# The start of the normed activations: from a multiple of 256 bytes to 192 bytes behind one

## Chip, cores and metric

The kernel runs on one core of one Trainium2 chip. The metric is the device time of one execution in microseconds; lower is better. A profile is taken in an execution of its own.

## What is computed

The reference is a decoder trunk of two layers on 256 tokens of width 1024, in float32. Each layer adds four blocks to x, each behind an RMS norm and with a second RMS norm on its output: a SwiGLU FFN (inner width 2816), a mixer, a cross-attention to 256 memory rows, and a second FFN. Layer 0 mixes with RWKV-7 (8 heads of 64) and retention (4 heads of 128) side by side, layer 1 with top-k sparse latent attention and a short convolution.

```python
for l in range(2):
    h = swiglu(rms_norm(x, ng[0]), w_gate[l, 0], w_up[l, 0], w_down[l, 0])
    x = x + 0.5 * rms_norm(h, ng[1])
    h = mixer(rms_norm(x, ng[2]))            # l = 0: rwkv7 | retention, l = 1: dsa | short conv
    x = x + rms_norm(h, ng[3])
    h = memory_xattn(rms_norm(x, ng[4]), rms_norm(mem, mem_norm_g), wq[l], wk[l], wv[l], wo[l])
    x = x + rms_norm(h, ng[5])
    h = swiglu(rms_norm(x, ng[6]), w_gate[l, 1], w_up[l, 1], w_down[l, 1])
    x = x + 0.5 * rms_norm(h, ng[7])
```

## The kernel before

Weights come from HBM in pieces of 512 KB (128 partitions x 1024 float32) into tiles wst. Each piece is split into two float32r tiles: whi, a copy by ScalarE (lines 196 and 239), and wlo, the rest wst - whi by VectorE (lines 197 and 245). Activations are split in the same way (split, lines 248 to 250). A product of two such pairs is three matmuls, hi x hi, hi x lo and lo x hi, into one PSUM bank (mm3, lines 254 to 256; project, lines 427 and 432, writes the same three in another order). Every matmul has a stationary operand of 128 columns, which a weight load brings in, and a moving operand of up to 512 columns.

The normed activations are called h here, and are the pair hhi, hlo, each 128 partitions x 8 k-tiles x 256 tokens of float32r. new_h (line 118) makes them. The class rms (line 313) fills them: it squares, scales, transposes in blocks of 128 x 128 (trh, line 351) and splits the result into hhi and hlo. There is one h for each norm ahead of a block, in the pools keep, memp, norm and hm. new_h is also called for o, the output of the cross-attention's values, and for y, the mixers' output; these take the place of an h in the pool keep.

h is read in two ways. group_t and proj_t hold the weights: whi or wlo, 128 of 256 columns, is stationary and a k-tile of h, 256 tokens, is moving. This is so for the FFNs' gate and up (pg, pu) in nine groups of 256 columns for each FFN, for the even mixer's input (pin), the memory keys (pk) and the convolution's inputs (pch, pcc, pcb). project, proj_nat and nat_both hold the activations: 128 tokens of a k-tile of h are stationary and 512 columns of weights (456 for pdi) are moving. This is so for the first 512 columns of each FFN's gate and up, for pq, pdi, prq, prv, prg and pvm. The FFN's down products (pd) and the output products (po) hold the act tiles, y or o and move 512 columns of weights.

In a group of an FFN (ffn, line 474) PE does 96 matmuls for gate and up and then 24 pd of the group before, while ScalarE and VectorE split the six weight pieces of the next ones. The weight loads are issued by SyncE as the staging tiles become free. Outside the stretches written under in_order, the tile framework orders each engine's instructions.

In the program's allocation all tiles of h, of the weights and of act start at a multiple of 256 bytes within the partition; below, such a multiple is called a line. A k-tile of h is 1024 bytes and a weight slice of 128 columns 512 bytes, so every operand of the matmuls above starts on a line. The one exception is pdi: its weight pieces have rows of 456 columns, so that the second k-tile of a piece starts 1824 bytes in, 32 bytes behind a line.

In the RWKV part front(c) handles one of four chunks of 64 tokens. It writes kr (line 948), which is squared on ScalarE and read for kn (line 963); later it writes bt (line 973) from kn, which BK reads (line 977). kr and bt have one buffer each, used by all four chunks in turn.

Of the kernel before, what the change touches and what calls it, by code (L numbers as in the profile page):

```python
# [10 lines left out]
F32 = mybir.dt.float32  # L11
F32R = mybir.dt.float32r
# [5 lines left out]
P = 128  # L18
S = 256
D = 1024  # L20
DT = D // P
# [73 lines left out]
def tile_hybrid_trunk(ctx: ExitStack, tc: tile.TileContext, a: dict, out: bass.AP, stop=None):  # L95
# [4 lines left out]
    keep = pool("keep")  # L100
# [8 lines left out]
    def bank(tag, name):  # L109
        return psum.tile([P, 512], F32, name=name, tag=tag)  # L110
# [4 lines left out]
    hneg = keep.tile([P, 4], F32, name="hneg")  # L115
    ones = keep.tile([P, 32], F32, name="ones")[:, 0:1]

    def new_h(p):
        return p.tile([P, DT, S], F32R, name="hhi", bufs=1), p.tile([P, DT, S], F32R, name="hlo", bufs=1)


    dram = pool("dram", space=bass.MemoryType.DRAM)
# [125 lines left out]
    def split(src, hi, lo):  # L248
        nc.scalar.activation(hi, src, AF.Copy)  # L249
        nc.vector.tensor_sub(lo, src, f32(hi))  # L250
# [50 lines left out]
    def power(dst, src, n):  # L301
        nc.gpsimd.tensor_tensor(dst, src, hneg[:, :n], op=ALU.pow)
# [294 lines left out]
    def cross(l, sp, y, w_unit, w_out, kts):  # L597

        wq, wo = a["xa_wq"][l], a["xa_wo"][l]
        wg, wu = a["ffn_w_gate"][l, 1], a["ffn_w_up"][l, 1]  # L600
        sc = 128.0 ** -0.5
        h, h2 = new_h(sp), new_h(sp)
        cx = ExitStack()
        xp = cx.enter_context(tc.tile_pool(reuse_waits="tile", name=f"xa{l}", bufs=1))
# [30 lines left out]
        with behind(env["loaded"]):  # L635
            nc.sync.dma_start(kT.rearrange("p a b -> p (a b)"), kd[l])
            nc.sync.dma_start(vM.rearrange("p a b -> p (a b)"), vd[l])
        gp2 = ng(l, 5)
        o = new_h(keep)
        pq, qn, qT, pr, mx, sm, pT, sps, nb = [{} for _ in range(9)]  # L640

        def query(t):
# [202 lines left out]
    def even_mixer(l, h, mh, mem_scope):  # L845
        i2 = l // 2
        w_in, w_out = a["ev_w_in"][i2], a["ev_w_out"][i2]
        with ExitStack() as cx:
            mp = cx.enter_context(tc.tile_pool(reuse_waits="tile", name="mix", bufs=1))
# [80 lines left out]
            t4 = lambda name, bufs=1: mp.tile([P, 4, 64], F32, name=name, bufs=bufs)  # L930
# [5 lines left out]
            def front(c):  # L936
                cs = slice(c * 64, (c + 1) * 64)
                inc = t4("inc")
                nc.vector.tensor_tensor_scan(fl(inc), fl(scan), fl(sig[:, c]), 0.0, op0=ALU.mult, op1=ALU.add)
                exc = mp.tile([P, 4, 64], F32, name="exc", tag="exc")  # L940
                nc.vector.tensor_sub(fl(exc), fl(inc), fl(sig[:, c]))
                e1, e2, e3 = t4("e1", 4), t4("e2"), t4("e3")
                nc.scalar.activation(e1, inc, AF.Exp, scale=-DECAY)
                nc.scalar.activation(e2, exc, AF.Exp, scale=-DECAY)
                nc.scalar.activation(e3, inc, AF.Exp, scale=DECAY)

                kr = t4("kr")
                nc.vector.tensor_mul(kr, kk[:, :, cs], pv[:, pvo["k_k"]:pvo["k_k"] + 4, None].to_broadcast([P, 4, 64]))
                sq = t4("sqk")
                nc.scalar.activation(sq, kr, AF.Square)  # L950
                ps = bank("fr", "prb")
                for f in range(4):
                    for hp, r in halves:
                        nc.tensor.matmul(ps[r, 256 + f:257 + f], sq[r, f, :], ones[r, :], start=True, stop=True)
                ssk = small.tile([P, 4], F32, name="ssk")
                nc.vector.tensor_scalar(ssk, ps[:, 256:260], 1e-24, None, op0=ALU.max)
                rin = small.tile([P, 4], F32, name="rin")
                power(rin, ssk, 4)
                dg = mp.tile([P, 4, 64], F32, name="dg", tag="sqk")
                nc.vector.tensor_mul(dg, idb, rin[:, :, None].to_broadcast([P, 4, 64]))  # L960
                nc.tensor.matmul(ps[:, 0:256], bones, fl(dg), start=True, stop=True)
                kn = t4("kn")
                nc.vector.tensor_mul(fl(kn), ps[:, 0:256], fl(kr))
                k2 = t4("k2")
                for f in range(4):
                    nc.scalar.activation(k2[:, f, :], av[:, c, f, :], AF.Identity, bias=omka[:, f:f + 1],
                                         scale=col("k_a", f))
                nc.vector.tensor_mul(k2, k2, kk[:, :, cs])
                KR = mp.tile([P, 4, 2, 64], F32, name="KR", bufs=4)
                nc.vector.tensor_mul(KR[:, :, 0, :], kn, e2)  # L970
                nc.vector.tensor_mul(KR[:, :, 1, :], rT[:, :, cs], e1)
                bt = t4("bt")
                nc.vector.scalar_tensor_tensor(fl(bt), fl(kn), -1.0, fl(e3), op0=ALU.mult, op1=ALU.mult)
                BK = mp.tile([P, 4, 2, 64], F32, name="BK")
                for hp, r in halves:
                    nc.vector.tensor_mul(BK[r, :, hp, :], k2[r], e3[r])
                    nc.vector.tensor_mul(BK[r, :, 1 - hp, :], bt[r], av[r, c])

                rk = mp.tile([P, 4, 64], F32, name="rk", tag="exc")
                nc.vector.tensor_mul(rk, rT[:, :, cs], k2)  # L980

                Q = mp.tile([P, 2, 4, 2, 64], F32, name="Q", bufs=4)
                for hp, r in halves:
                    ps = bank("fr", "pQ")
                    for f in range(4):
                        nc.tensor.matmul(ps[:, f * P:(f + 1) * P], fl(BK[r, f]), fl(KR[r, f]), start=True, stop=True)
                    nc.vector.tensor_mul(Q[:, hp].rearrange("p a k b -> p a (k b)"),
                                         ps.rearrange("p (a n) -> p a n", a=4),
                                         fl(cm)[:, None, :].to_broadcast([P, 4, P]))

                BKn = mp.tile([P, 4, P], F32, name="BKn", bufs=4)
                ps = bank("fr", "pBK")
                for f in range(4):
                    nc.tensor.transpose(ps[:, f * P:(f + 1) * P], fl(BK[:, f]), ident)
                nc.scalar.activation(fl(BKn), ps, AF.Copy)
                bn = small.tile([P, 4], F32, name="bn", bufs=4)
                ps = bank("fr", "pbn")
                for f in range(4):
                    for hp, r in halves:
                        nc.tensor.matmul(ps[r, f:f + 1], rk[r, f, :], col("r_k", f)[r, :], start=True, stop=True)  # L1000
                nc.vector.tensor_copy(bn, ps[:, 0:4])
                return e1, KR, Q, BKn, bn
# [144 lines left out]

            Sst = None
            fr = [front(i) for i in range(2)]
            U = [inverse(0, [z[2] for z in fr])]  # L1150
            for grp in (4, 5):
                shifted(grp)
            VV = [values(i) for i in range(4)]
            fr += [front(i) for i in range(2, 4)]
            U.append(inverse(1, [z[2] for z in fr[2:]]))
            for c in range(4):
# [8 lines left out]
            if mem_scope is not None:  # L1165
                mem_scope.close()
            y = retention(l, h, ya, cx)
        def w_unit(kt):
            if kt >= 4:
# [7 lines left out]
    def retention(l, h, ya, cx):  # L1177
# [54 lines left out]
        for t in range(2):  # L1232
            gates.append(r2("sgr"))
            nc.scalar.activation(fl(gates[t]), pss[t], AF.Silu)
        y = new_h(keep)
        split(ya, y[0][:, 0:4, :], y[1][:, 0:4, :])
        kv0 = r2("kv0")
        ps = bank("iv", "pkv")
        for i in range(4):
            o = slice(i * P, (i + 1) * P)  # L1240
# [3 lines left out]
        for t in range(2):  # L1244
            ps = bank("iv", "por")
            for i in range(4):
                o = slice(i * P, (i + 1) * P)
# [20 lines left out]
        for t in range(2):  # L1268
# [5 lines left out]
            o = (slice(None), slice(4, 8), slice(t * P, (t + 1) * P))  # L1274
# [4 lines left out]
    def odd_mixer(l, h, pss):  # L1279
        i2 = l // 2  # L1280
        w_in, w_out = a["od_w_in"][i2], a["od_w_out"][i2]
        with ExitStack() as cx:
# [60 lines left out]
            for t in range(2):  # L1343
                ts = slice(t * P, (t + 1) * P)
                n = (t + 1) * P
# [3 lines left out]
                for hh in range(0, 8, nb):  # L1349
# [7 lines left out]
                    for i in range(nb):  # L1357
                        k = order[hh + i]
# [18 lines left out]
                nc.vector.tensor_add(am[:, t * P:n], am[:, t * P:n], ntri)  # L1377
                amask.append(am)

            y = new_h(keep)  # L1380
            qlT = dp.tile([P, 8, S], F32, name="qlT")
            for hp in range(2):
                r = slice(hp * 64, hp * 64 + 64)
                for g in range(2):
# [4 lines left out]
                    k = 4 * g + hp  # L1389
                    nc.scalar.activation(qlT[:, k:k + 3:2, :], ps.rearrange("p (a n) -> p a n", a=2), AF.Copy)  # L1390
            sc_ = 64.0 ** -0.5
            for t in range(2):
                ts = slice(t * P, (t + 1) * P)
                n = (t + 1) * P
# [5 lines left out]
                for hh in range(0, 8, nb):  # L1400
# [8 lines left out]
                    for i in range(nb):  # L1409
                        k = hh + i  # L1410
# [23 lines left out]
                o = (slice(None), slice(0, 4), ts)  # L1434
# [157 lines left out]
    for l in range(depth):  # L1592
        if l % 2 == 0:
            y, w_unit = even_mixer(l, hm, mh if l == 0 else None, mem_scope if l == 0 else None)
            kts = [0, 1, 2, 3, 4, 5, 6, 7]
        else:
            y, w_unit = odd_mixer(l, hm, pss)
# [62 lines left out]
```

## Time and profile before

| | |
|---|---|
| median of 3 runs | 1223.0 us (1217.53 to 1226.41) |
| the profiled execution | 1217.95 us |
| its span, first to last instruction | 1216.1 us |
| granted TensorE clock over the span | 0.996 |
| PE (matmuls), PEld (weight loads) busy | 96%, 85% |
| DVE (VectorE), ACT (ScalarE), POOL (GpSimd) busy | 60%, 50%, 5% |
| moved by DMA | 213.99 MB, 176 GB/s on average |

Times in the rows are microseconds, those of one instruction nanoseconds. In a row "out<-moving,stationary" names the tiles; L256 is line 256. The start of an instruction is recorded; the end of a matmul is modelled, and matmuls are pipelined, so the distance from one start to the next is read as the cost of one, and a duration holds a tail that lies beside the next ones.

### The profile page before, as it was taken

The numbers are of one execution on the slowest core, as the hardware profiler recorded it, in microseconds if no ns is written. First come the engines' busy times: TensorE is split into PE (matmuls) and PEld (weight loads), VectorE is DVE, ScalarE is ACT, GpSimd is POOL, SyncE is SP. The second block draws the span as 40 slices with busy tenths as digits, with TensorE's granted clock in tenths as the row PEclk, the third lists the DMA queues.
The fourth block names the chain that finished last, engine by engine and source line by source line (L and its number), as shares of the span: only waits on it lengthen the run. The fifth ranks groups of instructions, "written<-read, shape, count | busy, mean of one in ns | idle before, by whom it ended". The sixth has DMA issues, their size and how long they took to land.

```text
span 1216.1 us, 19770 instructions
## 1 busy us (share of the span) xinstructions
PE 1168.7 (96%) x7956; PEld 1036.6 (85%) x7956; DVE 730.3 (60%) x1097; ACT 609.7 (50%) x908; POOL 65.0 (5%) x104
## 2 busy tenths in 40 slices
PE   6999999999899989999999999999899999999997
PEld 5899999997767767899999789999788777899996
DVE  5646555588647587755454755453669588644542
ACT  6546445754324567644443654443457467544441
POOL 0000000012231010000000000000100000000000
PEclk9999999999999999999999999999999999999999
DMA  6877655643553775576665486665432663766650
GB/s 220 244 255 225 189 179 165 198 144 103 164 138 86 223 262 156 165 217 181 197 182 168 141 242 191 189 185 157 137 88 87 221 213 120 229 202 192 184 164 35
DMA packets 152267, 213.99 MB, mean 176 GB/s; under 512 B 21872, under 2 KB 115184, under 8 KB 152176
## 3 DMA queue, kind: packets, MB, share of 16 engines
q1 hardware_dynamic: 138224, 206.58, 56.0%
q10 hardware_dynamic: 13216, 3.54, 1.2%
q0 software_dynamic: 736, 2.62, 0.6%
q8 instruction: 62, 1.02, 0.3%
q14 instruction: 29, 0.24, 0.1%
HBM read 206.67 MB, written 6.05 MB: 175 GB/s over the span
## 4 chain that ended last, share of the span: by engine, by line
PE 77%; DVE 9%; DMA 4%; ACT 4%; issue 3%; POOL 2%; SPq 0%; POOLq 0%; DVEq 0%; ACTq 0%
PE pd L254 6%; PE pd L255 6%; PE pd L256 6%; PE pg L256 6%; PE pg L255 6%; PE pu L255 6%; PE pu L254 6%; PE pg L254 6%; PE pu L256 6%; DVE wlo L197 1%; DVE wlo L245 1%; PE trh L351 1%; PE pin L256 1%; PE pin L254 1%; PE pin L255 1%
## 5 line engine op out<-in xcount | busy, mean ns | idle before, releaser
L197 DVE TENSOR_TENSOR wlo<-wst,whi 128x1024 fp32r<-128x1024 f32 x290 | 355.7, 1227 | 312.5 <-ACT whi L196 309.4
L196 ACT ACTIVATE whi<-wst 128x1024 fp32r<-128x1024 f32 x290 | 307.0, 1059 | 358.0 <-PE pg L255 81.9
L255 PE MATMUL pg<-hlo,whi 128*128 128x256 f32 x576 | 163.6, 284 | 0.0
L256 PE MATMUL pg<-hhi,wlo 128*128 128x256 f32 x576 | 163.6, 284 | 0.0
L254 PE MATMUL pg<-hhi,whi 128*128 128x256 f32 x576 | 163.2, 283 | 0.0
L254 PE MATMUL pu<-hhi,whi 128*128 128x256 f32 x576 | 163.0, 283 | 0.0
L255 PE MATMUL pu<-hlo,whi 128*128 128x256 f32 x576 | 163.0, 283 | 0.0
L256 PE MATMUL pu<-hhi,wlo 128*128 128x256 f32 x576 | 163.0, 283 | 0.0
L254 PE MATMUL pd<-whi,ahi 128*128 128x512 f32 x352 | 137.4, 391 | 0.0
L255 PE MATMUL pd<-wlo,ahi 128*128 128x512 f32 x352 | 137.1, 390 | 0.0
L256 PE MATMUL pd<-whi,alo 128*128 128x512 f32 x352 | 136.9, 389 | 0.0
L255 PEld LDWEIGHTS pg<-hlo,whi 128*128 128x128 f32 x576 | 110.9, 192 | 1.3
L254 PEld LDWEIGHTS pg<-hhi,whi 128*128 128x128 f32 x576 | 110.8, 192 | 1.3
L256 PEld LDWEIGHTS pg<-hhi,wlo 128*128 128x128 f32 x576 | 110.8, 192 | 0.0
L254 PEld LDWEIGHTS pu<-hhi,whi 128*128 128x128 f32 x576 | 110.6, 192 | 0.0
L255 PEld LDWEIGHTS pu<-hlo,whi 128*128 128x128 f32 x576 | 110.6, 192 | 0.0
L256 PEld LDWEIGHTS pu<-hhi,wlo 128*128 128x128 f32 x576 | 110.6, 192 | 0.0
L245 DVE TENSOR_TENSOR wlo<-wst,whi 128x1024 fp32r<-128x1024 f32 (+1 forms) x68 | 81.7, 1215 | 44.3 <-ACT whi L239 43.7
L239 ACT ACTIVATE whi<-wst 128x1024 fp32r<-128x1024 f32 (+1 forms) x68 | 70.2, 1052 | 36.3 <-PE pu L255 10.0
L256 PEld LDWEIGHTS pd<-whi,alo 128*128 128x128 f32 x352 | 66.1, 188 | 14.5 <-DVE alo L250 0.5
L254 PEld LDWEIGHTS pd<-whi,ahi 128*128 128x128 f32 x352 | 66.2, 188 | 13.2 <-ACT ahi L249 0.6
L255 PEld LDWEIGHTS pd<-wlo,ahi 128*128 128x128 f32 x352 | 66.2, 188 | 12.4
(374 smaller groups left out, 1992.5 us busy)
## 6 DMA issues: line engine op xcount, KB each, us to landing
wst<-in_ffn_w_gate_dram SPq DMA_DIRECT2D x88, 512.0 KB, 4.6
wst<-in_ffn_w_up_dram SPq DMA_DIRECT2D x88, 512.0 KB, 4.3
wst<-in_ffn_w_down_dram SPq DMA_DIRECT2D x88, 512.0 KB, 4.3
wst<-in_ev_w_in_dram SPq DMA_DIRECT2D x30, 512.0 KB, 3.9
gb<-in_norm_g_dram SPq DMA_DIRECT2D x16, 512.0 KB, 6.3
wst<-in_od_w_in_dram SPq DMA_DIRECT2D x12, 512.0 KB, 4.2
wst<-in_xa_wk_dram SPq DMA_DIRECT2D x8, 512.0 KB, 4.2
wst<-in_xa_wv_dram SPq DMA_DIRECT2D x8, 512.0 KB, 4.8
```

The costliest lines, as they stand in the source:

```text
L196: nc.scalar.activation(hi[:, :m], st[:, :m], AF.Copy)
L197: env["split"] = nc.vector.tensor_sub(lo[:, :m], st[:, :m], f32(hi[:, :m])).ins
L239: nc.scalar.activation(hi[:, :kt * n], st[:, :kt * n], AF.Copy)
L245: env["split"] = nc.vector.tensor_sub(lo[:, :m], st[:, :m], f32(hi[:, :m])).ins
L254: nc.tensor.matmul(ps, l_hi, r_hi, start=first, stop=False)
L255: nc.tensor.matmul(ps, l_hi, r_lo, start=False, stop=False)
L256: nc.tensor.matmul(ps, l_lo, r_hi, start=False, stop=last)
L351: nc.tensor.transpose(tr[:, i * P:(i + 1) * P], self.xg[q][:, i * P:(i + 1) * P], ident)
```

## The change

new_h takes 64 elements more for each of the two tiles and hands out a view that starts 48 elements, 192 bytes, in. For y and o the shift is 0, so they start on a line as before, in the larger tile. All other tiles stay on the lines. In the RWKV part kr and bt share one buffer (the tag kr), which takes 1024 bytes less of each partition. No instruction is added or removed.

```diff
-    def new_h(p):
-        return p.tile([P, DT, S], F32R, name="hhi", bufs=1), p.tile([P, DT, S], F32R, name="hlo", bufs=1)
+    def new_h(p, shift=48):
+
+        return tuple(p.tile([P, DT * S + 64], F32R, name=name, bufs=1)[:, shift:shift + DT * S].rearrange(
+            "p (k n) -> p k n", k=DT) for name in ("hhi", "hlo"))
...
-        o = new_h(keep)
+        o = new_h(keep, 0)
...
-                kr = t4("kr")
+                kr = mp.tile([P, 4, 64], F32, name="kr", tag="kr")
...
-                bt = t4("bt")
+                bt = mp.tile([P, 4, 64], F32, name="bt", tag="kr")
...
-        y = new_h(keep)
+        y = new_h(keep, 0)
...
-            y = new_h(keep)
+            y = new_h(keep, 0)
```

## Rows read from the trace of the kernel before

**Rows 1.** The page, part 1: busy us (share of the span) and instructions.
```profile
PE 1168.7 (96%) x7956; PEld 1036.6 (85%) x7956; DVE 730.3 (60%) x1097; ACT 609.7 (50%) x908; POOL 65.0 (5%) x104
```

**Rows 2.** The page, part 4: the chain that ended last, by engine.
```profile
PE 77%; DVE 9%; DMA 4%; ACT 4%; issue 3%; POOL 2%; SPq 0%; POOLq 0%; DVEq 0%; ACTq 0%
```

**Rows 3.** Busy time by stretches: length, engines (instructions), clock, DMA share, GB/s.
```profile
30.00:60.00 30.00, 27.81 (x166) 25.18 (x165) 18.78 (x20) 15.51 (x18) 0.00 (x0) 0.94 0.82 247
60.00:215.00 155.00, 155.00 (x1084) 145.31 (x1083) 86.25 (x95) 77.22 (x104) 3.12 (x5) 1.00 0.66 201
...
500.00:530.00 30.00, 28.86 (x177) 25.77 (x176) 19.24 (x19) 16.32 (x18) 0.00 (x0) 1.00 0.77 233
530.00:640.00 110.00, 110.00 (x771) 103.43 (x771) 54.44 (x51) 48.03 (x51) 0.00 (x0) 1.00 0.65 190
...
700.00:720.00 20.00, 18.66 (x130) 17.33 (x129) 12.47 (x13) 10.66 (x12) 0.00 (x0) 1.00 0.82 254
720.00:840.00 120.00, 120.00 (x847) 113.10 (x846) 59.31 (x56) 52.76 (x56) 0.00 (x0) 1.00 0.66 192
...
1030.00:1070.00 40.00, 39.20 (x230) 34.50 (x229) 25.28 (x25) 21.19 (x24) 0.00 (x0) 1.00 0.68 210
1070.00:1195.00 125.00, 125.00 (x894) 118.28 (x893) 59.22 (x56) 51.92 (x57) 0.00 (x0) 1.00 0.58 169
```

**Rows 4.** Timeline of PE in an FFN group, first and last of 36 starts.
```profile
99.79 0.28 PE L255 MATMUL pg<-hlo,whi 128*128 128x256 f32 x1
...
103.99 0.28 PE L254 MATMUL pu<-hhi,whi 128*128 128x256 f32 x1
```

**Rows 5.** The f32 matmuls psc: eight in the timeline, and durations (min/median/max).
```profile
460.31 1.89 PE L660 MATMUL psc<-kT,qT 128*128 128x256 f32 x8
```
```profile
L660 PE MATMUL psc<-kT,qT x32: 377/379/414, 460.3 to 1004.6; 128*128 128x256 f32 x32
```

**Rows 6.** pdi in the timeline at either clock; the stretch at the lower clock.
```profile
872.55 0.37 PE L427 MATMUL pdi<-whi,hhi 128*128 128x456 f32 x1
...
873.78 0.37 PE L427 MATMUL pdi<-whi,hhi 128*128 128x456 f32 x1
```
```profile
879.53 0.58 PE L427 MATMUL pdi<-wlo,hhi 128*128 128x456 f32 x1
...
881.43 0.96 PE L432 MATMUL pdi<-whi,hlo 128*128 128x456 f32 x2
```
```profile
879.30:882.50 3.20, 3.20 (x10) 2.80 (x9) 1.51 (x5) 0.60 (x5) 0.70 (x1) 0.50 0.01 3
```

**Rows 7.** Line 254 from 100 to 200 us: durations in ns, min/median/max.
```profile
L254 PEld LDWEIGHTS pu<-hhi,whi x96: 192/192/192, 103.9 to 195.9; 128*128 128x128 f32 x96
...
L254 PE MATMUL pg<-hhi,whi x91: 277/283/363, 100.0 to 190.3; 128*128 128x256 f32 x91
L254 PEld LDWEIGHTS pd<-whi,ahi x47: 186/188/192, 109.6 to 200.0; 128*128 128x128 f32 x47
```

**Rows 8.** Groups of matmuls by line and shape; each stands on three lines.
```profile
L255 PE MATMUL pg<-hlo,whi 128*128 128x256 f32 x576 | 163.6, 284 | 0.0
...
L255 PE MATMUL pu<-hlo,whi 128*128 128x256 f32 x576 | 163.0, 283 | 0.0
...
L255 PE MATMUL pin<-hlo,whi 128*128 128x256 f32 x112 | 31.9, 285 | 0.0
...
L255 PE MATMUL pk<-hlo,whi 128*128 128x256 f32 x64 | 18.3, 287 | 0.0
...
L255 PE MATMUL pcc<-hlo,whi 128*128 128x256 f32 x32 | 9.8, 305 | 0.0
```

**Rows 9.** Groups of ScalarE by line and shape: the eviction of h.
```profile
L249 ACT ACTIVATE hhi<-trh 128x512 fp32r<-128x512 f32 x36 | 20.4, 595 | 8.2 <-PE trh L351 8.0
```

**Rows 10.** Timeline of VectorE where the second chunk follows the first.
```profile
259.91 0.86 DVE L977 TENSOR_TENSOR BK<-bt,av 64x256 f32<-64x256 f32 x2
260.81 0.42 DVE L948 TENSOR_TENSOR kr<-kk,pv 128x256 f32<-128x256 f32 x1
```

## The prediction

> **What bounds the kernel now.** I read the busy line of the page first: TensorE's matmuls fill 1168.7 of 1216.1 us, VectorE 60%, ScalarE 50% [rows 1]. The chain that ended last says the same: 77% of it is PE [rows 2]. Then busy time by stretches [rows 3]: in the four long FFN stretches PE is busy all of 155, 110, 120 and 125 us, 510 us together, while the DMA engines are at 0.58 to 0.66. In the four stretches ahead of them (30 to 60, 500 to 530, 700 to 720, 1030 to 1070 us) PE has holes (27.81 of 30, 28.86 of 30, 18.66 of 20, 39.20 of 40) and the DMA engines stand at 0.68 to 0.82: there the weights are late. So in the long stretches the time is a number of matmuls times their spacing, and nothing else.
>
> A busy PE is not a PE at its rate, so the spacing has to be looked at. In the timeline, 35 steps of the 256-column matmuls of pg and pu take 103.99 - 99.79 = 4.20 us, that is 120.0 ns each [rows 4]. 256 columns at the granted 2.4 GHz are 106.7 ns, so 13.3 ns of each step are no streaming. Three other rows say what this piece is. The f32 matmuls psc, also 256 columns, stand further apart: eight of them take 1.89 us up to an end that lies 379 ns after the last start, so (1.89 - 0.379) / 7 = 215.9 ns. That is twice 106.7 and 2.5 more, so their columns pass at half the rate and the excess is only 2.5 ns [rows 5]. The 456-column matmuls pdi run at both clocks: at 2.4 GHz six steps take 873.78 - 872.55 = 1.23 us, 205 ns each, 15 over the 190 of the columns; while the granted clock was 0.50, that is 1.2 GHz, five steps take 881.43 - 879.53 = 1.90 us, 380 each, which is 456 columns and nothing more [rows 6]. So the excess is not a fixed cost of changing weights (it would stay at half clock and with f32): it appears only where the moving operand is read at its highest rate, beside the weight load of the next matmul. And the loads feel it too: in pu every load takes 192 ns, in pd 188 in the median [rows 7]. I take the excess for the two reads of one matmul pair disturbing each other.
>
> **What the change moves.** It touches three things.
>
> (a) The start of h. Of the instructions that read hhi and hlo as the moving operand there are 3 x 576 pg, 3 x 576 pu, 3 x 112 pin, 3 x 64 pk and 9 x 32 pch, pcc and pcb: 4272, all of 256 columns [rows 8]. Before, both streams start on a line; after, the moving one starts 192 bytes behind one. Whether that separates the reads is not shown by any row, so I bound it. Best end: the excess falls to what psc shows, 2.5 ns, a step of 109.2 ns, 10.8 less. Worst end: pdi. There the second k-tile of a weight tile starts 456 x 4 = 1824 bytes in, that is 32 bytes behind a line, so half of these moving reads are off the lines, and the mean excess is 15 to 15.5 instead of 13.3: if the off-line half carries it all, 2 x 2.2 = 4.4 ns more each. One row suggests that the excess does depend on how the two streams meet: the shortest pg matmul lasts 277 ns, 6 less than the 283 of nearly all others [rows 7]. (These are the first of a group behind pd, where the load stands otherwise to the stream.) That is a step of 114. I take the middle between 114 and 109.2, some 111.6, so 8.4 ns less per matmul, and keep 109.2 and 124.4 as ends. The row of 277 is the nearest, since it is the same matmul on the same tiles, met at another moment.
>
> [...]
>
> Not all 4272 can be gained. In the four stretches with late weights PE would only wait longer. They hold 166 + 177 + 130 + 230 = 703 matmuls [rows 3], of which some 80% are the 256-column kind (96 pg and pu to 24 pd in a group of an FFN): 562. That leaves 3710 x 8.4 ns = 31.2 us. What covers the rest: in the long stretches the loads would have to come 7% faster, a DMA share of 0.62 to 0.71, below the 0.77 to 0.82 that the late stretches reach; VectorE is busy 86 of 155 us there and ScalarE 77, so neither is late next.
>
> (b) h as the stationary operand: pq 4, pdi 2, prq 4, prv 2, prg 2, pvm 4 and the first 512 columns of gate and up of four FFNs 16, which makes 34 blocks of one token half, each of 8 k-tiles x 3 = 24 matmuls, 816 of 456 or 512 columns. The weight load shifts, the stream stays on the lines. The ends are -10.8 ns (all of it gone) and +4.4 as in pdi: -8.8 to +3.6 us. Nearest is the pdi row, but there it is the stream that is off the lines, so I take 0. pd and po, stationary ahi or y and o, stay as they were: the change gives y and o a shift of 0.
>
> (c) Writes of h and memory. The 36 evictions hhi<-trh take 595 ns each [rows 9]; if an off-line start cost each of them and its hlo partner on VectorE a tenth of that, 36 x 0.12 = 4.3 us at most, much of it beside PE's other matmuls; taken as 0. kr and bt now share one buffer. That adds a wait: the next chunk's kr may not be written before BK has read bt. In the trace this order already holds: BK<-bt at 259.91 for 0.86 us, the next kr at 260.81, on the same engine [rows 10], and the other two pairs lie alike. Queued behind kr on VectorE are KR and the splits wlo, which PE wants for pin, but as kr stands behind BK anyway nothing moves: cost 0, and if it were late, 3 times the 0.42 us of a kr, 1.3 us. No matmul, transfer or eviction is added or removed. The pools shift by some hundred bytes; waits at their seams may move by a microsecond or two either way.
>
> **The sum.** The profiled execution took 1217.95 us, 1.85 more than its span; 1217.95 - 31.2 = 1186.8. The median of the runs shown, 1223.0, lies 5.05 above the profiled one; with that the forecast is 1192 us, 2.5% less. Its own range, from the first gain that a measurement can tell (1%, 12.2 us, a saving of 3.3 ns for each of 3710) to the best end for all 4272 + 816 (54.9 us), is 1168 to 1211. About 1% is what a measurement of this kernel tells from no change.
>
> **Rivals.**
> First, nothing happens: the excess is a property of f32r matmuls beside a load, whatever the address. For it: 120.0 holds for every k-tile and every buffer of four FFNs, although their distances vary by many multiples of 256 bytes. Against it: all of these are the same modulo 256, and the row of 277. Time: 1223, give or take 6.
> Second, slower. The moving row of 1024 bytes, now off the lines, touches five lines where it touched four, and each step pays for the fifth, as half of pdi's do. Price 4.4 ns on 4272 matmuls, 18.8 us, so 1242; it decides from 2.9 ns (12.2 us / 4272) on. For it: the mean of pdi. Against it: 456 columns are no whole number of lines, so that the excess may come from the length; and 192 is a whole number of 64-byte pieces, 32 is not.
> Third, the spacing falls but the weights bind: the loads arrive at 169 to 201 GB/s in the long stretches and 210 to 254 in the late ones; if the late stretches grow to twice their length, half of the gain goes: 1207. Against it: the DMA share above.
>
> **Chances.** Forecast 0.46, third rival (a gain too) 0.08, nothing 0.26, slower 0.20. So faster by over 1%: 0.54; within 1%: 0.26; slower by over 1%: 0.20. The range goes from the best end, 1168, up to 1236, with the no-change case inside and the dearer half of the slower case outside: some 0.15 is left out.
>
> **What would show it.** Right: in the timeline of the long stretches pg and pu steps of 109 to 115 ns (the matmuls last 272 to 278 instead of 283), pd unchanged, loads of pu back from 192 towards 188, the long stretches shorter by some 5%, a higher DMA share in them. Wrong: steps of 120.0 as before (first rival), of 123 or more (second), or short steps with new holes in PE and more waits of whi on transfers (third). If the steps of pq, prq or the first pg of an FFN change, part (b) was not 0. If kr stands late behind BK with PE idle after it, part (c) was wrong.

## The result, and the profile after

| | before | after |
|---|---|---|
| median of 4 runs each, on one chip | 1220.99 us (1217.53 to 1226.41) | 1206.03 us (1204.22 to 1208.03) |
| the profiled execution | 1217.95 us | 1206.94 us |
| its span | 1216.1 us | 1205.1 us |
| ratio after to before | | 0.9874, 95% interval 0.983 to 0.9917 |

The kernel became 1.3% faster; 2.5% had been forecast. The sign and the place were right, the size of one term was three times too large. In a second series of six runs (e7) the gain was 1.0%.

The page of after, parts 1 and 4, answers to [rows 1, 2]:

```profile
PE 1159.0 (96%) x7956; PEld 1025.9 (85%) x7956; DVE 729.5 (61%) x1097; ACT 610.0 (51%) x908; POOL 65.0 (5%) x104
...
PE 76%; DVE 9%; DMA 5%; ACT 5%; issue 3%; POOL 2%; SPq 0%; POOLq 0%; DVEq 0%; ACTq 0%
```

PE is busy for 1168.7 - 1159.0 = 9.7 us less. The rest of the span, in which PE had holes, went from 1216.1 - 1168.7 = 47.4 to 1205.1 - 1159.0 = 46.1 us. So nearly all of the 11.0 us is shorter matmul steps, and no new holes have come in their place. The long FFN stretches say so too (busy time by stretches, columns as in [rows 3]):

```profile
60.00:215.00 155.00, 154.99 (x1113) 145.49 (x1112) 87.77 (x97) 80.34 (x109) 4.26 (x10) 1.00 0.68 207
530.00:640.00 110.00, 110.00 (x799) 104.24 (x798) 55.66 (x52) 49.34 (x53) 0.00 (x0) 1.00 0.65 190
...
720.00:840.00 120.00, 120.00 (x864) 113.37 (x863) 59.09 (x56) 53.27 (x57) 0.00 (x0) 1.00 0.64 189
```

PE is as full as it was, and in the same time it gets through more matmuls: 1113 instead of 1084, 799 instead of 771, 864 instead of 847, which is 2 to 4%. (How many of a window's matmuls are the 512-column kind differs, so the steps from start to start are the cleaner reading.)

The timeline of PE in the same FFN group as in [rows 4], first and last of 36 starts:

```profile
99.75 0.28 PE L257 MATMUL pg<-hlo,whi 128*128 128x256 f32 x1
...
103.87 0.28 PE L256 MATMUL pu<-hhi,whi 128*128 128x256 f32 x1
```

35 steps in 4.12 us are 117.7 ns, where it was 120.0. But one group later there is another rate:

```profile
112.50 1.04 PE L353 MATMUL trh<-ident,xn 128*128 128x128 f32 x8
113.29 0.37 PE L256 MATMUL pg<-hhi,whi 128*128 128x256 f32 x1
113.50 0.28 PE L257 MATMUL pg<-hlo,whi 128*128 128x256 f32 x1
...
116.45 0.28 PE L256 MATMUL pg<-hhi,whi 128*128 128x256 f32 x1
```

From 113.50 to 116.45 there are 26 steps, 113.5 ns each. These matmuls differ from those at 99.75 in nothing but what went before: here eight transposes (trh) stand between the last pd and the first pg. Of the 4193 steps of h-moving matmuls that are shorter than 150 ns, 3554 are 117 to 119 ns and 600 are 113 to 114; of the 36 FFN groups of 96 matmuls, 32 run at 117.8 and 4 at 113.4, each from its first few matmuls to its last. All 30 groups that follow pd directly are among the 32; the other six begin their long run behind transposes, four of them at the quicker rate. In before 3977 of 4188 steps were 120. The mean step of pu fell from 120.0 to 117.3 ns, that of pg from 120.6 to 117.7.

Lines 256 and 258 (254 and 256 before) from 100 to 200 us, minimum/median/maximum as in [rows 7]:

```profile
L256 PEld LDWEIGHTS pu<-hhi,whi x96: 187/188/188, 101.3 to 191.3; 128*128 128x128 f32 x96
L256 PE MATMUL pu<-hhi,whi x96: 276/281/281, 101.4 to 191.4; 128*128 128x256 f32 x96
...
L258 PEld LDWEIGHTS pu<-hhi,wlo x96: 187/192/192, 101.5 to 191.5; 128*128 128x128 f32 x96
```

The loads went from 192 to 188 ns, as the prediction wanted, but on two of the three lines only: in the 30 groups behind pd the load of the third product still takes 192 (in the two others at 117.8 it is that of another product), and only in the quicker groups do all three take 188. The matmuls went from 283 to 281 or, in the quicker groups, 276. A step can be read from a duration: 283 goes with 120.0, 281 with 117.8, 276 with 113.3, 163 ns less each time. The groups of matmuls:

```profile
L257 PE MATMUL pg<-hlo,whi 128*128 128x256 f32 x576 | 161.7, 281 | 0.0
...
L256 PE MATMUL pd<-whi,ahi 128*128 128x512 f32 x352 | 137.1, 390 | 0.0
...
L257 PE MATMUL prg<-wlo,hhi 128*128 128x512 f32 x16 | 6.3, 394 | 0.0
```

pg went from 284 [rows 8] to 281. pd, whose operands did not move, has a mean step of 227.5 (228.2 before). prg, one of those where h is stationary, became longer (389 before).

So the time is made up like this: 4272 matmuls with h moving, 2.7 ns less each, 11.5 us less; 816 with h stationary, some 2 ns more each (pu 229.4 to 231.4, prg 226.7 to 229.0, pq 237.5 to 238.6 in the mean), 1.6 us more; together 9.9 us, beside the 9.7 by which PE's busy time fell. (So close an agreement is partly luck: 0.7 ns on each of 1056 pd are not in the sum, and the profiles differ in where the granted clock was 0.5, at 39.5 and 879.2 us before and at 320, 337 and 962 us after, for 3.4 us each time; either moves the sum by a microsecond or so.) Left to explain: why 2.7 and not 8.4, and what decides between 117.8 and 113.4.

### The profile page after: what moved, and what is told of

Its sections match the earlier page's. It is cut to its first block, busy times and chain, and to the rows that moved or that the text cites. A ratio compares the mean times of both kernels' runs of the same rounds, so it can differ in the third digit from the quotient of the medians.

```text
span 1205.1 us, 19769 instructions
## 1 busy us (share of the span) xinstructions
PE 1159.0 (96%) x7956; PEld 1025.9 (85%) x7956; DVE 729.5 (61%) x1097; ACT 610.0 (51%) x908; POOL 65.0 (5%) x104
## 4 chain that ended last, share of the span: by engine, by line
PE 76%; DVE 9%; DMA 5%; ACT 5%; issue 3%; POOL 2%; SPq 0%; POOLq 0%; DVEq 0%; ACTq 0%
PE pd L256 6%; PE pd L258 6%; PE pd L257 6%; PE pg L258 6%; PE pg L256 6%; PE pu L256 6%; PE pg L257 6%; PE pu L257 6%; PE pu L258 6%; DVE wlo L247 2%; DVE wlo L199 1%; PE trh L353 1%; POOL rstd L304 1%; ACT whi L198 1%; ACT sq L326 1%
## 5 line engine op out<-in xcount | busy, mean ns | idle before, releaser
L256 PEld LDWEIGHTS pg<-hhi,whi 128*128 128x128 f32 x576 | 108.2, 188 | 1.3
L257 PEld LDWEIGHTS pg<-hlo,whi 128*128 128x128 f32 x576 | 108.2, 188 | 1.3
```

Source lines behind the costliest of these rows:

```text
L256: nc.tensor.matmul(ps, l_hi, r_hi, start=first, stop=False)
L257: nc.tensor.matmul(ps, l_hi, r_lo, start=False, stop=False)
```

## Experiments

**A map of the two starts.** e1 leaves the trunk out: it runs only blocks of 48 f32r matmuls, one for each pair of starts of the moving operand (a to h: 0, 32, ... 224 bytes behind a line) and of the stationary one, with 256 and with 512 columns.

```diff
+            for s in range(8):
+                for m in range(8):
+                    c += 1
+                    run("n_m" + L[m] + "_s" + L[s], 8 * m, 8 * s, 256, c)
```

> This kernel leaves out the whole trunk and returns x with a column added; it holds only float32r matmuls in the order of group_t (hi, lo, hi against two weight tiles, 48 in a block), one block for each of 64 pairs of starts: moving operand 0, 32, ... 224 bytes and stationary operand 0, 32, ... 224 bytes behind a line, first with 256 and then with 512 columns. Theory A (the distance of the two streams modulo 256 bytes decides): the spacing is constant along the diagonals of the map; at (0, 0) 120.0 ns for 256 columns, at (192, 0) 117 to 118, at (224, 32) and (0, 64) the same as at (192, 0). Theory B (only the start of the moving operand decides): the spacing is constant along a column of the map, (192, s) is 117 to 118 for every s and (0, s) is 120.0. Theory C (neither; the spacing falls into one of several states for reasons of its own): no order by the offsets, and the same pair can give 114 or 118 in two blocks. For 512 columns A and B expect 226.7 at (0, 0) and a change of 2 to 3 ns with the offset; as the kernel's own 512-column matmuls with shifted h went from 227 to 229, A expects (0, 192) at 229.

Steps in ns, mean of the last 36 of a block, in order of the distance (start of the moving operand minus start of the stationary one, modulo 256 bytes). Each distance was met at eight pairs of starts; the 512-column row is that of the stationary operand on a line.

| distance, bytes | 0 | 32 | 64 | 96 | 128 | 160 | 192 | 224 |
|---|---|---|---|---|---|---|---|---|
| 256 columns | 120.0 | 117.8 | 117.8 | 120.0 | 118.6 to 118.8 | 118.6 four times, 117.3 four times | 117.8 six times, 113.3 twice | 118.2 |
| 512 columns | 226.7 | 233.3 | 228.9 | 233.3 | 233.3 | 234.2 | 233.3 | 233.3 |

Groups of matmuls of e1 (n has 256 columns, w 512; then the letters of the moving and the stationary start):

```profile
L43 PE MATMUL w_ma_sb<-h,w 128*128 128x512 f32 x48 | 11.4, 395 | 0.0
...
L43 PE MATMUL w_ma_sg<-h,w 128*128 128x512 f32 x48 | 11.1, 391 | 0.0
...
L43 PE MATMUL w_ma_sa<-h,w 128*128 128x512 f32 x48 | 11.1, 389 | 0.0
...
L43 PE MATMUL n_ma_sa<-h,w 128*128 128x256 f32 x48 | 5.9, 283 | 0.0
...
L43 PE MATMUL n_mb_sb<-h,w 128*128 128x256 f32 x48 | 5.9, 283 | 0.0
...
L43 PE MATMUL n_mg_sa<-h,w 128*128 128x256 f32 x48 | 5.8, 281 | 0.0
...
L43 PE MATMUL n_mf_sh<-h,w 128*128 128x256 f32 x48 | 5.6, 276 | 0.0
```

Two things follow. The distance of the two starts counts, and at six of the eight distances nothing else did in this map, whose starts all lie on multiples of 32 bytes: with both 32 bytes behind a line (n_mb_sb) the step is that of both on the line, 120.0 ns, although every moving row of 1024 bytes then lies on five lines instead of four. The second rival falls with that. And the wide matmuls go the other way: for them distance 0 is the best (226.7 ns), 64 costs 2 ns (228.9) and the others 6 or 7 (233.3 to 234.2). n_mg_sa is the pair of the changed kernel in pg and pu. w_ma_sg is that of its matmuls with h stationary: 192 bytes for the stationary operand is a distance of -192, that is 64, and the row has the 2 ns that pu and prg lost. n_mf_sh and n_mb_sd have the same distance as n_mg_sa and yet 276 (steps of 113.3): either the absolute start counts there, or what ran before. The two values at 160 ask the same. And as each block stood behind only one other, a value of the map is a rate that the distance showed there; the map doesn't say that it is the only one.

That the two reads of a matmul pair get into each other's way would fit the map (120.0 ns at distance 0, 117.8 at 64), but no run shows the reads.

**The shift alone, at other values.** e2, e3 and e4 are the changed kernel with new_h at 0, 64 and 128 bytes; all else of the change, the shared buffer of kr and bt included, stays.

```diff
-    def new_h(p, shift=48):
+    def new_h(p, shift=0):
```

(16 in e3, 32 in e4.)

> The changed kernel with a shift of 0: larger tiles of h, pools moved, kr and bt in one buffer, but every h on a line. If the gain comes from the start of h alone: as before, 1221 us, ratio to before 0.995 to 1.005, steps of 120.0. If it comes from the other placement of the pools or from the shared buffer: 0.987, as the change.

> The changed kernel with h 64 bytes behind a line. Theory A with an effect that is even in the distance (64 and 192 are both 64 from a line): 117 to 118 ns and 0.987 as the change. Theory A with an odd effect: a step of 120 or more, ratio 1.0 or above. Theory C: either, without order.

> The changed kernel with h 128 bytes behind a line, the farthest from the weights' lines. If the distance separates the reads, it should do most here: steps of 109 to 115 ns and a ratio of 0.97 to 0.985. If what counts is only not to be at 0: 117 to 118 and 0.987. If 192 is a place of its own: 120 and 1.0.

| | shift | median | ratio, 95% interval |
|---|---|---|---|
| e2 | 0 | 1219.09 us | 0.9996 (0.9974 to 1.0019) |
| e3 | 64 bytes | 1215.38 us | 0.9964 (0.9946 to 0.9981) |
| e4 | 128 bytes | 1218.59 us | 0.9994 (0.9969 to 1.0018) |

The groups of pu in e2, in e3 (with one where h is stationary, and with pcb) and in e4:

```profile
L256 PE MATMUL pu<-hhi,whi 128*128 128x256 f32 x576 | 163.0, 283 | 0.0
```

```profile
L256 PE MATMUL pu<-hhi,whi 128*128 128x256 f32 x576 | 161.2, 280 | 0.0
...
L429 PE MATMUL pu<-whi,hhi 128*128 128x512 f32 x40 | 16.0, 401 | 0.0
...
L256 PE MATMUL pcb<-hhi,whi 128*128 128x256 f32 x32 | 8.8, 276 | 0.0
```

```profile
L258 PE MATMUL pu<-hhi,wlo 128*128 128x256 f32 x576 | 163.8, 284 | 0.0
...
L256 PE MATMUL pu<-hhi,whi 128*128 128x256 f32 x576 | 161.9, 281 | 0.0
```

e2 has the steps and the time of before: the gain is the start of h, and the shared buffer and the shifted pools give and cost nothing that can be measured. e3 wins nearly as much on pg and pu as the change (117.8 ns), but there h as the stationary operand stands at distance 192, and those wide steps rise from 229.4 to 235.4: 4272 x 2.2 = 9.4 us gained, 816 x 6.0 = 4.9 us lost, 4.5 left, and 0.0036 x 1219.41 = 4.4 us were measured. Most steps of its pcb, at the same distance of 64, took 113 to 114 ns, where e1 has 117.8 for 64 in all eight blocks: so that distance has more than one rate too. e4's three products go apart, 281 for one and 284 for the others, so that pu's mean gains 0.3 ns; the wide steps lose as in e3, and no difference in time was measured. 192 bytes is the best of the values tried because the change's two uses of h, moving and stationary, get 192 and 64 out of it (117.8 and 228.9 ns), which are the cheapest pair in the map.

**Start or entry?** e5 asks whether the absolute start decides between 117.8 and 113.3. Again the trunk is left out: distance 192 at eight starts in four orders, each block behind one like pd, and then a scan of the distance in steps of 16 bytes, with the stationary operand 0, 16, 32 and 96 bytes behind a line.

```diff
+            for r in range(4):
+                for i in range(8):
+                    s = (i, 7 - i, 3 * i % 8, 5 * i % 8)[r]
+                    c += 1
+                    run("pd", 0, 0, 512, c, 4)
+                    c += 1
+                    run("r" + L[r] + "_s" + L[s], (8 * s + 48) % 64, 8 * s, 256, c)
```

> Leaves out the trunk as the first map did. In the first map the spacing followed the distance of the two starts, but at a distance of 192 two of eight pairs ran at 113.3 ns and the others at 117.3 to 117.8; both had the stationary operand 96 bytes behind a multiple of 128. Here a distance of 192 stands at all eight starts, four times each in four orders, each behind a short block of 512-column matmuls with distance 0, as pd stands ahead of pg in the kernel. Theory D (the absolute start has a share): the starts at 96 and 224 give 113.3 in all four orders, the others 117 to 118. Theory E (a block falls into one of two states by how it was entered): 113 and 118 appear at any start, or everywhere the same because the entry is the same. The rest is a scan of the distance in steps of 16 bytes at four starts: if lines of 32 bytes or more are what counts, a step of 16 bytes gives the value of a neighbour; for 512 columns only distance 0 gives 226.7 and the others 229 to 234.

Groups of e5: r blocks of the first order with the stationary start at 0 (sa) and 96 bytes (sd), the scan's block at distance 192 with it at 0 (dm_ta), and two at distance 112 with it at 16 (dh_te) and 0 (dh_ta):

```profile
L43 PE MATMUL dh_te<-h,w 128*128 128x256 f32 x48 | 5.9, 284 | 0.0
...
L43 PE MATMUL ra_sa<-h,w 128*128 128x256 f32 x48 | 5.8, 281 | 0.0
...
L43 PE MATMUL ra_sd<-h,w 128*128 128x256 f32 x48 | 5.6, 277 | 0.0
...
L43 PE MATMUL dm_ta<-h,w 128*128 128x256 f32 x48 | 5.6, 276 | 0.0
...
L43 PE MATMUL dh_ta<-h,w 128*128 128x256 f32 x48 | 5.6, 275 | 0.0
```

The r blocks looked like a proof of theory D, the absolute start: starts 96, 160 and 224 ran at 113.3 in all four orders, the other five at 117.8. The scan takes it back. There the block before was one of 256 columns at distance 176, and start 0, slow behind pd, ran at 113.3 like the others. And the scan answered a second question: over all sixteen distances nothing is below 113.3, which 112 bytes reached too. It also bounds what e1 said of the distance. With the stationary operand 0, 32 or 96 bytes behind a line each distance gave the same step; with it 16 bytes behind one, the steps are others: 118.3 instead of 120.0 at distance 0, 120.0 instead of 113.3 at 112. So at starts off the multiples of 32 bytes the distance alone doesn't decide.

e6 asks the same of the kernel: weights 96 bytes behind a line and h 32, still a distance of 192, with y, o and the cross-attention's h put at distance 0 to their partners.

```diff
+    wpool.tile([P, 24], F32, name="fillw", bufs=1)
...
-        h, h2 = new_h(sp), new_h(sp)
+        h, h2 = new_h(sp, 0), new_h(sp)
...
-        o = new_h(keep, 0)
+        o = new_h(keep, 24)
...
-    mh = new_h(memp)
+    mh = new_h(memp, 8)
```

(y as o, hm as mh.) e7 is the changed kernel itself, timed again beside it.

> The changed kernel with a filler of 96 bytes ahead of the weights' pool, so that the weights start 96 bytes behind a line, and every h that moves starts 32 bytes behind one: the distance is 192 as in the change, but neither stream is where it was; h that is stationary alone, y and o have the weights' start (distance 0). Theory A says as the change, 117 to 118 ns and 0.987. Theory D says 113.3 ns: 4.2 ns less on 4272 matmuls, 18 us, so about 0.973. If the absolute start of the moving operand alone decided: neither 0 nor 192, so no forecast but not 117.5. The matmuls with pq go back from 229 to 226.7.

> The changed kernel once more, on the same chip as the one before it and with the same runs of the kernel before: 0.983 to 0.992, steps of 113 to 118 ns with a mean of 117.3 in pu. If the mix of states is a matter of how each block is entered in one execution, the share of steps at 113 to 114 differs from that of the first profile; if it is fixed by the addresses, it is the same to the percent.

```profile
L257 PE MATMUL pu<-hhi,whi 128*128 128x256 f32 x576 | 161.4, 280 | 0.0
```

This group of e6 is that of after. e6 took 1211.33 us, 0.9926 (0.99 to 0.9953), with some 22% of its steps at 113 to 114; e7 1208.3 us, 0.9903 (0.987 to 0.9936), with 468 steps at 113 to 114 where the first profile had 600. Theory D expected nearly all of e6's steps at 113.3. It falls: with weights and h at the starts that were quick in e5, all 30 groups that follow pd directly run at 117.8, as in after and e7; the weights of pd stand at the new start too here, while in e5 the block like pd stayed on the line. Of the six groups that begin behind transposes all six are quick in e6, and four in e7 as in after, but not the same four. e7 also says that the share of quick steps isn't the same in every execution.

**Which entries lead to 113.3.** e8, without the trunk again, runs a block like pd and behind it a block like pg at distance 192, with sixteen ways from the one to the other in three orders (gx, gy, gz), and four of them at distance 0 (gw).

```diff
+        cases = {"a": (W, None, {}), "b": ([256, 256], None, {}), "c": ([384, 128], None, {}), ...
+                 "e": ([128] * 4, None, {}), "f": (W, 32, {}), "g": (W, 64, {}), "h": (W, 128, {}), "i": (W, "t", {}),
+                 "j": (W, None, {"split": (128, 128)}), "k": (W, None, {"split": (192, 64)}), ...
```

> Leaves out the trunk, as the maps did. Each case is a block of 24 matmuls of 512 columns at distance 0 (as pd) and then a block of 48 of 256 columns at distance 192 (as pg); between them stands something else in each of 16 cases, and every case stands three times, in three orders. Theory E (the state of a block is set by how it is entered and held to its end): case a, nothing between, gives 117.8 all three times, as nearly all groups of the changed kernel do; some of the others (the last 512 columns done as two, three or four pieces, a short matmul or a transpose put between, the first 256 columns in two halves, another order of the three products) give 113.3, and each gives the same all three times. If the state were drawn by chance, the three would differ; if 117.8 belonged to the distance and 113.3 to something else in the kernel, all would be 117.8. The last four blocks stand at distance 0: 120.0 whatever the entry, if distance 0 has one state alone.

Groups of e8: a, nothing between; b, the last 512 columns of pd as 256 + 256; j, the first 256 of pg as 128 + 128:

```profile
L39 PE MATMUL gw_vb<-h,w 128*128 128x256 f32 x48 | 5.9, 283 | 0.0
L39 PE MATMUL gw_va<-h,w 128*128 128x256 f32 x48 | 5.9, 283 | 0.0
...
L39 PE MATMUL gy_vi<-h,w 128*128 128x256 f32 x48 | 5.9, 283 | 0.0
...
L39 PE MATMUL gx_va<-h,w 128*128 128x256 f32 x48 | 5.8, 281 | 0.0
...
L39 PE MATMUL gx_vi<-h,w 128*128 128x256 f32 x48 | 5.7, 278 | 0.0
...
L39 PE MATMUL gx_vb<-h,w 128*128 128x256 f32 x48 | 5.6, 276 | 0.0
...
L39 PE MATMUL gx_vj<-h,w 128*128 128x256 f32 x47 | 5.6, 277 | 0.0
```

a ran at 117.8 in all three orders; b and j at 113.3 in all three. So did c, d and n (the last matmul cut unevenly, the short piece last), k (the first one cut as 192 + 64) and g (one matmul of 64 columns put between). p (the last one cut as 64 + 448), e (the last one in four), l (another order of the three products) and matmuls of 16, 32, 128 or 256 columns between changed nothing (117.8). i, a transpose between, is the only one that differs from order to order: 113.3, 117.8 and 113.3 once it is steady (its rows of 278 and 283 hold its first, longer steps too). At distance 0, with both on a line, all four entries tried gave one rate, 120.0: gw_vb is gw_va. So at distance 192 a block had two lasting rates, 117.8 and 113.3, and the matmuls at its entry chose between them. The weight loads tell the rates apart: in the steady part of every block at 113.3 all loads take 188 ns in the median, and at 117.8 one of three takes 192. Which one it is goes with the entry too: the third product's load in a, the second's in e, f, h and m, the first's in o. At distance 0 all three take 192.

**The entry in the kernel.** e9 is the changed kernel with the last pd matmul of each block of pd cut in two; e10 the kernel before with the same cut; e11 the changed kernel with the first pg matmul of each group cut in two. Each cut computes the same sums; each half brings in its weights again, so a cut also adds a weight load: the pages count 7988 in e9 and e10 and 7992 in e11, where before and after have 7956.

```diff
-        nc.tensor.matmul(ps, l_lo, r_hi, start=False, stop=last)
+        if cut:
+            nc.tensor.matmul(ps[:, :256], l_lo, r_hi[:, :256], start=False, stop=False)
+            nc.tensor.matmul(ps[:, 256:], l_lo, r_hi[:, 256:], start=False, stop=last)
+        else:
+            nc.tensor.matmul(ps, l_lo, r_hi, start=False, stop=last)
...
-                        down(ac, i, kt, t, u)
+                        down(ac, i, kt, t, u, cut=t == 1 and kt == todo[-1][2])
```

(e11: the same in the first product of mm3, as ps[:, :128] and ps[:, 128:], where group_t makes pg.)

> The changed kernel; of each pd block inside an FFN's loop the last matmul is done as two of 256 columns. Theory E: 30 of the 36 groups of pg and pu are entered from pd, 26 or 27 of them at 117.8 in the changed kernel; they now run at 113.3. 96 matmuls x 4.4 ns = 0.42 us a group, 30 x 0.42 = 12.7 us, less some 13 ns for each of 30 cuts (0.4 us): 1194 us, ratio to before 0.979. If the state of a block in the kernel is set by something else (traffic, the splits beside it): 117.8 as before and 1206 to 1208, ratio 0.988 to 0.991.

> The same cut in the kernel before, with every start on the lines. Distance 0 has one state, 120.0, whatever the entry: 1221 us, ratio 0.998 to 1.002, steps of 120. If the cut itself were what helps, the gain of the cut would be here too: 0.99.

> The changed kernel; instead of the last pd, the first matmul of each pg group is done as two of 128 columns. Theory E: the same state, 113.3, in all groups entered from pd; the entry alone measured 20 ns less than with the cut pd. 1193 to 1194, ratio 0.979. If the entry from pd in the kernel differs from that of the bare blocks: 1206 to 1208.

| | median | ratio, 95% interval | mean step of pu |
|---|---|---|---|
| e9, after with the last pd cut | 1196.36 us | 0.9806 (0.9782 to 0.9829) | 113.5 ns |
| e10, before with the last pd cut | 1218.59 us | 0.9987 (0.997 to 1.0004) | 120.0 ns |
| e11, after with the first pg cut | 1200.54 us | 0.9831 (0.9805 to 0.9856) | 114 ns |

The group of pu in e9, in e10 and in e11:

```profile
L256 PE MATMUL pu<-hhi,whi 128*128 128x256 f32 x576 | 159.1, 276 | 0.0
```

```profile
L254 PE MATMUL pu<-hhi,whi 128*128 128x256 f32 x576 | 163.0, 283 | 0.0
```

```profile
L260 PE MATMUL pu<-hhi,whi 128*128 128x256 f32 x576 | 159.4, 277 | 0.0
```

The timeline of PE in e9 where a group is entered:

```profile
128.64 0.39 PE L257 MATMUL pd<-wlo,ahi 128*128 128x512 f32 x1
128.87 0.28 PE L259 MATMUL pd<-whi,alo 128*128 128x256 f32 x1
128.98 0.28 PE L260 MATMUL pd<-whi,alo 128*128 128x256 f32 x1
129.10 0.29 PE L256 MATMUL pg<-hhi,whi 128*128 128x256 f32 x1
129.22 0.28 PE L257 MATMUL pg<-hlo,whi 128*128 128x256 f32 x1
...
130.93 0.28 PE L257 MATMUL pg<-hlo,whi 128*128 128x256 f32 x1
```

The two halves of pd take 129.10 - 128.87 = 0.23 us, some 6 ns more than a whole one, and the 15 steps from 129.22 to 130.93 are 114 ns, the first of them 121, the second 116 and the rest 113 to 114. In e9 and in e11 all 30 groups that follow pd directly run at 113.3 once they are steady, where all 30 ran at 117.8. One matmul ahead of each group cut in two, without any other work moved, brings pg and pu from 117.5 to some 114 ns, and the kernel from 0.9874 and 0.9903 to 0.9806. PE's busy time in e9's profile is 1143.2 us, 25.5 less than before, and its holes are 1188.9 - 1143.2 = 45.7 us. (Some 2 of the 25.5 us are clock, an estimate from before's profile, in which eight steps of pdi took 380 ns instead of 206 and some of the first pg 214 instead of 120 at a granted clock of 0.5; in e9's profile the clock stays up until 3.5 us before the end.) The cut without the shift does nothing (e10). e9 is faster than both kernels: the slowest of its six runs, 1199.43 us, is below the fastest of the changed kernel's ten, 1204.22. e11 had been expected at 1193 to 1194 us and came out 7 us above. A part of that shows in its profile: five of the six groups behind transposes ran at 117.8 (one in e9), and the cut groups behind pd start with steps of some 173 and 116.

## Why the prediction was right, and where it was not

**What bounds the kernel: right.** The FFN stretches stayed full, and the time moved by number of matmuls times change of step.

**What the excess is: right in kind.** The 13.3 ns are what lies above 106.7, and that is an estimate: 456 columns took 380 ns at a granted clock of 0.50 [rows 6], which at twice the clock would be 190, 2.4 columns a ns, and 106.7 for 256; pg's 214 ns for 256 columns at 0.50 agree. The 2.4 GHz of the prediction stand for that rate; no run shows the clock in GHz. The 13.3 ns were laid to the two reads of a matmul pair meeting; no run shows the reads themselves. e1 shows that the step depends on the distance of their starts modulo 256 bytes; e5 adds that the starts count too when they are no multiples of 32 bytes, and e8 that the entry does. Two of three loads of pu fell from 192 to 188 as predicted. But only a part of the 13.3 ns hangs on the address: 6.6 stay at the best distance (113.3). The first rival, nothing, falls with e2 beside after: the one number 48 or 0 makes the difference.

**Step (a), the price per matmul: the step that failed.** 8.4 ns was taken, 2.7 was measured; 4272 x 2.7 = 11.5 us stand where 31.2 stood. That 1206 lies inside 1168 to 1236 is no merit of this step, since that range holds a gain, no change and a loss alike. The middle between 114 and 109.2 had two flaws. The end at 109.2, taken over from the f32 matmuls, is not reached at any of the sixteen distances in e5: of the 13.3 ns the best pair gives back 6.7 (120.0 to 113.3). And the row of 277 ns was no rate at all. Timelines of PE behind pd, before and after:

```profile
98.24 0.28 PE L254 MATMUL pg<-hhi,whi 128*128 128x256 f32 x1
98.35 0.28 PE L255 MATMUL pg<-hlo,whi 128*128 128x256 f32 x1
98.47 0.28 PE L256 MATMUL pg<-hhi,wlo 128*128 128x256 f32 x1
```

```profile
95.74 0.28 PE L256 MATMUL pg<-hhi,whi 128*128 128x256 f32 x1
95.86 0.28 PE L257 MATMUL pg<-hlo,whi 128*128 128x256 f32 x1
```

In before every group that follows pd has one step of 113 or 114, then one of 119 or 120, and then 120.0 to its end; in after its first step is 117 or 118. The prediction had noted that those matmuls are the first behind pd, "where the load stands otherwise to the stream", and then counted on them for every matmul. That 113.3 turned up as a lasting rate in four groups is another matter; nothing in before pointed to it, and that it agrees with the 114 of the prediction is luck. The steady rate of a group entered from pd is 117.8. Where the entry is changed (e9), the mean gain is 6.5 ns for pu, still under 8.4.

**The deduction for late weights: not needed.** 562 of 4272 matmuls were left out of the sum because PE would wait longer there. The holes of PE did not grow, from 47.4 to 46.1 us in after and 45.7 in e9, and PE's busy time fell by what all 4272 and the 816 make: in e9 the mean step below 150 ns went from 119.9 to 114.1, 4272 x 5.8 - 1.6 = 23.2 us, and with the 2 us of clock that is 25.2, with 25.5 seen. From the start of an FFN to its first group behind pd, which takes in the late stretch, the second to fourth FFN took 47.7, 48.8 and 47.4 us in before, 47.4, 48.2 and 46.8 in after and 46.9, 48.2 and 46.7 in e9. No run varied the loads alone there.

**Step (b): inside its bounds, but not 0.** With h stationary each wide matmul costs some 2 ns more, 1.6 us in all. The row taken as nearest, pdi, had a sign of it: with half of its moving reads 32 bytes behind a line its mean excess was 15 to 15.5 ns, and e1 shows 6.6 ns more at that distance than at 0 with 512 columns (233.3 and 226.7). No row of before showed that the narrow and the wide matmuls want different distances. The second rival used the same row for the narrow ones; its five lines have no effect in e1, and the 64-byte pieces named against it none on 256 columns there (117.8 ns at distance 32 as at 64).

**Step (c): right.** e2 has the shared buffer and the moved pools without the shift, at 0.9996; the 36 evictions hhi<-trh take 595 ns in after as in before, off the line as on it. The order of kr behind BK holds in after as in [rows 10] (timeline of VectorE):

```profile
266.24 0.86 DVE L979 TENSOR_TENSOR BK<-bt,av 64x256 f32<-64x256 f32 x2
...
267.48 0.42 DVE L950 TENSOR_TENSOR kr<-kk,pv 128x256 f32<-128x256 f32 x1
```

**The third rival, weights that bind: not seen.** The DMA share in the first three long stretches is 0.64 to 0.68 against 0.65 to 0.66 before, with PE full, and 0.52 against 0.58 in the last; the higher share that the prediction named as a sign did not come. Even e9, with some 25 us gained to the changed kernel's 12 to 15, shows no added holes.

**What stays open.** That the entry chooses the rate is shown, in bare blocks and in the kernel; why a cut of 256 + 256 chooses the quicker one and four pieces of 128 don't is not. Why the transpose between gives now one and now the other, and why the share of quick steps differs between executions of one kernel, is not settled either; small differences in when the first loads run may do it, but no run varied that alone. In e5 the starts 96, 160 and 224 were quick each time behind the same block, so that how a run's starts lie to those of the block ahead may belong to the entry; no run tested that by itself.

## What to carry to other kernels

Read the step from start to start and compare it with half of what the same columns take at half the granted clock (here 205 ns at 1.00, and 380 at 0.50, for 456 columns [rows 6]). Where an excess is left, try the distance of the two operands' starts modulo 256 bytes; measure it in the kernel and for each width, since one distance had more than one rate (117.8 and 113.3 ns at 192), and 256 columns were slowest at 0 (120.0 ns) where 512 columns were quickest (226.7). Before the gain is multiplied by the number of matmuls, check in the timeline that the short step is a rate that a whole group holds, and not that of the few matmuls where it was met. Where a block has two lasting rates, try its entry: here cutting one matmul in two ahead of each group took pg and pu from 117.5 to some 114 ns and the kernel from 1206 to 1208 us down to 1196, nearly as much again as the addresses had given.

## What the runs showed of the hardware that was not expected

- A run of f32r matmuls of 256 columns at distance 192 had two steady rates, 117.8 and 113.3 ns; the rate that it had after its first few matmuls it kept to its end, over 96 matmuls in an FFN group and over 153 of pin in after. At distance 0, on lines, only 120.0 was seen to last (e8, e10).
- The order of the distances turned round with the width: 512 columns took 226.7 ns at distance 0, 228.9 at 64, and 232 to 234 at the others; 256 columns were slowest at 0 and 96, both 120.0 (e1).
- A 512-column matmul cut into two of 256 cost some 6 ns at the end of pd (0.23 us for both, e9), and 32 such cuts in the kernel before left its time at 0.9987 (0.997 to 1.0004, e10).
- A weight load beside a 256-column matmul lasted 192 ns for all three products at distance 0 (120.0), at distance 192 for one of three at 117.8 and for none at 113.3 (e8, and all 36 FFN groups each of after, e6, e7, e9 and e11). It is no measure of the step elsewhere: e1 has loads of 188 in the median with steps of 120.0 at distance 96.
